# Second mixer: its convolution as column-group products, with TensorE in a written-out order

## The chip, the core and the metric

The kernel runs on one core of one Trainium2 chip. The metric is the device time of one execution in microseconds (us). Times of instructions are those of one execution recorded by the hardware profiler. TensorE (PE in the rows) multiplies, with PEld its weight loads; VectorE (DVE) and ScalarE (ACT) do the elementwise work; GpSimd (POOL) does small powers; SyncE (SP) issues the weight transfers.

## What is computed

Two networks run one after the other on 256 rows of width 1024. The first has a state-space mixer, a feed-forward block, an attention mixer and another feed-forward block. The second puts 16 meta rows ahead of the 256 rows, runs one mixer and then a block with 16,384 experts. Only the second network's mixer is touched by the change. Cut to what matters:

```python
def conv_group(a, b, conv_w, conv_b, g_ln, b_ln):          # 512 channels, 31 taps
    h = a * jax.nn.sigmoid(b)
    h = lax.conv_general_dilated(h, conv_w[:, None, :], window_strides=(1,),
                                 padding=[(CONV_K - 1, 0)], feature_group_count=CONV_CH, ...) + conv_b
    h = layernorm(h, g_ln, b_ln)
    return jax.nn.silu(h)

z = rmsnorm_2(h, g_mix_norm) @ w_in
conv_out = conv_group(z[..., :512], z[..., 512:1024], conv_w, conv_b, g_conv_ln, b_conv_ln)
attn_out = mla_group(z[..., 1024:1280], z[..., 1280:1408], z[..., 1408:], pos, ...)   # 8 heads, causal softmax
mixed = jnp.concatenate([rmsnorm_2(attn_out, g_out_attn), rmsnorm_2(conv_out, g_out_conv)], axis=-1)
h = h + mixed @ w_out
```

## The kernel before

Activations are kept transposed, 1024 features as 8 groups of 128 partitions by 256 rows (272 with the meta rows), and the rows are otherwise handled as two tiles of 128. Each weight piece of 128 x 1024 comes in over SyncE's queue into one of four buffers and is split by `weight` (line 120) into a high part (ScalarE, line 128) and a low part (VectorE, line 129). Each product is then three matmuls in a split-precision type: `mm_a` (lines 139 to 141, a weight piece as the stationary operand, 256 or 272 columns) or `mm_b` (lines 145 to 147, activations as the stationary operand, up to 512 columns). Attention, convolution and transposes run in plain f32; every f32 matmul is two records in the trace. `to_T` (line 164) transposes a tile on TensorE and splits it (lines 171, 133, 134).

`mix2` (line 782) is the stage of the change. `low_rank` (line 867) computes 416 columns of queries, keys, values and rotary part for three row tiles (two of 128 and one for the 16 meta rows); `ab(f)` (line 802) computes the gated values of 128 channels, for f from 0 to 3; `queries` and `key_values` expand the low-rank parts to 8 heads and turn them; `scores`, `flip` and `values` (lines 961 to 991) are one head's attention over one row tile, 16 in all; `attn_done` and `conv_done` norm the two halves and turn them into the operand `mT` of the output projection `out_proj` (line 239), which is 8 weight pieces, the first four for the attention half.

The convolution of a channel block is split. On TensorE, `taps_pe` builds a 128 x 128 diagonal for each tap on ScalarE (line 821) and multiplies it by a shifted view of the gated values (line 822). On VectorE, `taps_v` does one multiply-add per tap (line 829). The constant says how many taps TensorE has for each block:

```python
PE_TAPS = (4, 4, 6, 31)
```

So 45 taps are on TensorE and 79 on VectorE. The softmax of a row is two exponentials (lines 972 and 973), because the probabilities of the 16 meta keys are kept in a part of their own that is padded to 128; their sums are added by line 975.

The order is a planner's: the pieces are traced in an order that `weave` makes out of two lists, and a scheduler then orders every engine's queue by its own estimate of when operands are ready. `defer` and `tick` move the second half of a norm some pieces later. The stage ends:

```python
run(low_rank() + B[0])
weave([queries] + B[1] + [key_values], C[0])
weave(S, B[2] + C[1] + B[3] + C[2])      # S: attention, C: taps, B: ab
load_gain("ffn2_g")
run(C[3])
flush()
o = out_proj(A["w_out2"], KD, mT, keep_tiles(sb, 3, "qT2"))
conv_done(0)
conv_done(1)
```

## Time and profile before

| | |
|---|---|
| median of 3 runs | 1710.59 us (1710.31 to 1714.95) |
| the profiled execution, its own time | 1710.3 us |
| its span, first to last instruction | 1708.5 us |
| TensorE busy | 1669.0 us (98%) |
| VectorE busy | 1259.0 us (74%) |
| ScalarE busy | 964.7 us (56%) |
| mean granted TensorE clock | 0.996 of full |

The span is what the instructions cover; 1.8 us lie around it. Busy times of TensorE overlap, since a matmul's record runs to its modelled end while the next has begun: the distance from one start to the next tells what a matmul costs the queue. The second mixer runs from 777.5 us to about 900 us.

### The profile page before, as it was taken

Reading aid. Unit: us, or ns where it says so; the run is one execution under the profiler, and the core shown is the slowest. Engines: PE = TensorE matmul, PEld = TensorE weight load, DVE = VectorE, ACT = ScalarE, POOL = GpSimd, SP = SyncE. Lnnn points to the kernel's source line nnn. Section 1 sums busy time; section 2 is a strip of 40 time slices with the busy share of each in tenths; the row PEclk is TensorE's granted clock in tenths of the full one; section 3 lists DMA queues with packets and bytes.
Section 4 is the critical chain, followed back from the end, with each engine's and each line's share of the span. In section 5 each row is a group of like instructions: output and inputs, shape, how many; then the busy total and the mean of one; then the engine's idle time right before and its main releaser. Section 6 shows DMA issues by size and latency. Waiting matters only on the chain.

```text
span 1708.5 us, 28836 instructions
## 1 busy us (share of the span) xinstructions
PE 1669.0 (98%) x11003; PEld 1488.0 (87%) x11003; DVE 1259.0 (74%) x2581; ACT 964.7 (56%) x1425; POOL 37.6 (2%) x49
## 2 busy tenths in 40 slices
PE   6999999999999999999999999999999999999998
PEld 6978779997777799988988999999999888888886
DVE  5777667765765677757986998999999766666665
ACT  5688556544455665546765454556666544444443
POOL 0000000000100000001000000000000000000000
PEclk9999999999999999999999999999999999999999
DMA  5534445566354356664334666765555677777774
GB/s 192 183 119 141 136 148 182 188 197 199 118 177 134 116 174 185 208 212 145 103 99 160 229 221 218 230 226 174 182 177 178 214 239 237 235 232 242 237 241 151
DMA packets 88492, 315.30 MB, mean 185 GB/s; under 512 B 10001, under 2 KB 11409, under 8 KB 88225
## 3 DMA queue, kind: packets, MB, share of 16 engines
q1 hardware_dynamic: 80352, 290.36, 53.1%
q10 hardware_dynamic: 8000, 23.09, 3.7%
q8 instruction: 86, 1.41, 0.3%
q14 instruction: 54, 0.43, 0.1%
HBM read 295.59 MB, written 17.83 MB: 183 GB/s over the span
## 4 chain that ended last, share of the span: by engine, by line
PE 90%; DVE 4%; ACT 2%; issue 1%; DMA 1%; POOL 1%; SPq 0%; DVEq 0%; POOLq 0%; ACTq 0%
PE mm L1265 21%; PE mm L139 13%; PE mm L141 13%; PE mm L140 13%; PE mm L145 7%; PE mm L146 7%; PE mm L147 7%; PE pst L1224 3%; PE pst L171 1%; DVE lo L129 1%; PE pst L724 1%; PE pst L546 1%; PE po L749 1%; PE mm L822 1%; ACT hi L128 0%
## 5 line engine op out<-in xcount | busy, mean ns | idle before, releaser
L129 DVE TENSOR_TENSOR lo<-raw,hi 128x1024 fp32r<-128x1024 f32 (+1 forms) x492 | 599.6, 1220 | 289.6 <-PE mm L1265 81.2
L128 ACT ACTIVATE hi<-raw 128x1024 fp32r<-128x1024 f32 (+1 forms) x492 | 519.4, 1057 | 496.9 <-PE mm L140 220.8
L139 PE MATMUL mm<-xT,hi 128*128 128x256 f32 (+1 forms) x1968 | 562.3, 286 | 1.2 <-DVE cacc L320 1.2
L141 PE MATMUL mm<-xT,lo 128*128 128x256 f32 (+1 forms) x1968 | 556.6, 283 | 1.9 <-DVE lo L129 1.9
L140 PE MATMUL mm<-xT,hi 128*128 128x256 f32 (+1 forms) x1968 | 551.2, 280 | 0.0
L139 PEld LDWEIGHTS mm<-xT,hi 128*128 128x128 f32 x1968 | 371.5, 189 | 3.9 <-issue 2.3
L141 PEld LDWEIGHTS mm<-xT,lo 128*128 128x128 f32 x1968 | 370.1, 188 | 2.9 <-DVE lo L129 2.5
L140 PEld LDWEIGHTS mm<-xT,hi 128*128 128x128 f32 x1968 | 371.1, 189 | 0.7
L1265 PE MATMUL mm<-hi,xT 128*128 128x512 f32 x992 | 270.0, 393 | 0.0
L1265 PEld LDWEIGHTS mm<-hi,xT 128*128 128x128 f32 x992 | 186.3, 188 | 42.6
L1265 PE MATMUL mm<-lo,xT 128*128 128x512 f32 x496 | 154.7, 392 | 0.0
L1265 PEld LDWEIGHTS mm<-lo,xT 128*128 128x128 f32 x496 | 93.1, 188 | 21.6
L145 PE MATMUL mm<-hi,xT 128*128 128x512 f32 (+1 forms) x240 | 95.9, 406 | 4.4 <-ACT xT L133 3.8
L146 PE MATMUL mm<-lo,xT 128*128 128x512 f32 (+1 forms) x240 | 95.7, 399 | 2.2 <-DVE lo L129 2.2
L147 PE MATMUL mm<-hi,xT 128*128 128x512 f32 (+1 forms) x240 | 94.8, 396 | 2.1 <-DVE xT L134 2.1
L320 DVE SCALAR_TENSOR_TENSOR cacc<-mm,pcol,cacc 128x255 f32<-128x255 f32 (+1 forms) x144 | 68.4, 480 | 12.9 <-ACT cacc L317 10.4
L1225 ACT ACTIVATE G<-pst 128x512 f32<-128x512 f32 x64 | 68.3, 1106 | 0.0
L1215 DVE TENSOR_TENSOR oo<-oo,slot 128x1536 bf16<-128x1536 bf16 x64 | 61.2, 956 | 1.7
L145 PEld LDWEIGHTS mm<-hi,xT 128*128 128x128 f32 x240 | 45.2, 190 | 14.5 <-ACT xT L133 5.4
L147 PEld LDWEIGHTS mm<-hi,xT 128*128 128x128 f32 x240 | 45.3, 189 | 12.2 <-DVE xT L134 4.1
L146 PEld LDWEIGHTS mm<-lo,xT 128*128 128x128 f32 x240 | 45.5, 190 | 11.5 <-DVE lo L129 4.0
L145 PE MATMUL mm<-hi,aT 128*128 128x512 f32 x136 | 53.9, 396 | 0.0
(409 smaller groups left out, 2115.0 us busy)
## 6 DMA issues: line engine op xcount, KB each, us to landing
raw<-in_u SPq DMA_DIRECT2D x128, 512.0 KB, 4.1
raw<-in_v SPq DMA_DIRECT2D x128, 512.0 KB, 4.3
raw<-in_w_up SPq DMA_DIRECT2D x88, 512.0 KB, 3.6
raw<-in_w_dn SPq DMA_DIRECT2D x44, 512.0 KB, 4.2
raw<-in_w_fox SPq DMA_DIRECT2D x32, 512.0 KB, 4.2
spill<-h ACTq DMA_DIRECT2D x30, 512.0 KB, 5.5
h<-spill SPq DMA_DIRECT2D x30, 512.0 KB, 4.8
raw<-in_w_xbc SPq DMA_DIRECT2D x24, 512.0 KB, 3.7
```

The source lines that it names most:

```text
L128: last[1] = nc.scalar.activation(hi[:, :width], raw[:, :width], AF.Copy)
L129: last[0] = nc.vector.tensor_tensor(lo[:, :width], raw[:, :width], hi[:, :width].bitcast(F32), op=OP.subtract)
L139: nc.tensor.matmul(ps, lhsT=hi[:, k, :], rhs=xT[:, k, 0, :], start=(k == 0), stop=False)
L140: nc.tensor.matmul(ps, lhsT=hi[:, k, :], rhs=xT[:, k, 1, :], start=False, stop=False)
L141: nc.tensor.matmul(ps, lhsT=lo[:, k, :], rhs=xT[:, k, 0, :], start=False, stop=(k == nk - 1))
L145: nc.tensor.matmul(ps, lhsT=xT[:, k, 0, c0:c1], rhs=whi, start=first, stop=False)
L146: nc.tensor.matmul(ps, lhsT=xT[:, k, 0, c0:c1], rhs=wlo, start=False, stop=False)
L147: nc.tensor.matmul(ps, lhsT=xT[:, k, 1, c0:c1], rhs=whi, start=False, stop=last)
L320: nc.vector.scalar_tensor_tensor(acc[:, d:], ps[:, :T - d], cw[:, j:j + 1], acc[:, d:], op0=OP.mult, op1=OP.add)
L1215: nc.vector.tensor_tensor(oo[:, 2:], oo[:, 1:2].to_broadcast([P, 3, P, NB]), cur[:, 2:, None].to_broadcast([P, 3, P, NB]), op=OP.mult)
L1225: nc.scalar.activation(G[:, :, t0:t0 + NB].rearrange("p i t -> p t i"), pg, AF.Copy)
L1265: nc.tensor.matmul(acc[2 * t + c], lhsT=w[x][:, t * P:(t + 1) * P], rhs=y[:, c, :], start=(i == 0 and x == 0 and y is b[0]), stop=(i == P ...
```

## The change

The convolution moves to TensorE as a whole. Each block of 128 channels is handled as four column groups of 32 channels. The gated values are written to DRAM and read back as four copies shifted by one row each, laid out so that the 128 partitions of one operand are 32 channels times 4 shifts; one matmul with a stationary operand of 128 x 32 does four taps of 32 channels, and its output goes to 32 of the 128 PSUM partitions. Eight such steps cover 32 taps (31 and a zero). The stationary tables are laid out on the host side of the layout function, like the weights, and come from DRAM in two transfers, so that ScalarE builds no diagonals and VectorE has no taps.

The softmax becomes one exponential over the whole row: the first block of keys is taken as 128 columns that overlap the next, and the values of the meta tile are zero beyond row 16. The low-rank projection computes for the meta tile only the 160 columns that are used. TensorE's queue is in program order for the stage (`manual_schedule`), with an explicit list `fill` of what stands between the attention steps. Weight pieces are loaded and split one ahead of use (`plan`, `pre`). The output projection takes the four convolution pieces first, and two of them are placed in attention steps 16 and 17. The diff, cut to its core:

```diff
-PE_TAPS = (4, 4, 6, 31)
-CD = 0
+NTAP = 8
+CD = 1
...
+    pre, plan = [], []
+
     def weight(src, shape, width=PIECE, keep=None):
+        if pre:
+            s, w = pre.pop()
+        else:
+            w = load(src, shape, width, keep)
+        if plan:
+            pre.append((plan[0][0], load(*plan.pop(0))))
+        return w
...
-    def out_proj(src, nk, yT, keep, fin=residual):
+    def out_proj(src, nk, yT, keep, fin=residual, order=None):
+        order = order or list(range(nk))
...
+            def diagonals():
+                for p in range(2):
+                    d = sb.tile([P, 2, 4 * NTAP, 32], F32, name=f"dg{p}")
+                    nc.scalar.dma_start(d, A["c2d"][p])
+                    DG[2 * p], DG[2 * p + 1] = d[:, 0], d[:, 1]
...
                     pb = a_block(A["w_ab"][f, 1], xT)
...
-                    nc.vector.tensor_tensor(U[f][:, CONV_K - 1:], pre[0], sg, op=OP.mult)
+                    nc.vector.tensor_tensor(u[:, CONV_K - 1:UW - 1], first[0], sg, op=OP.mult)
+
+                    d = dram.tile([P, UW], F32, name=f"cud{f}")
+                    nc.gpsimd.dma_start(d, u)
+                    V[f] = sb.tile([P, 4, UW - 3 - NM], F32, name="cv", bufs=2)
+                    for s in range(4):
+                        nc.gpsimd.dma_start(V[f][32 * s:32 * s + 32],
+                                            d[:, NM + s:UW - 3 + s].rearrange("(q c) t -> c q t", q=4))
...
-            def taps_pe(f, j0, j1):
+            def taps(f, m0, m1):
+                if m0 == 0:
                     CP[f] = ps_mm.tile([P, 512], F32, name="mm")[:, :T]
-                dg = sb.tile([P, j1 - j0, P], F32, name="dg", bufs=2)
-                for j in range(j0, j1):
-                    nc.scalar.activation(dg[:, j - j0, :], ident, AF.Copy, scale=col("c2w", f * CONV_K + j))
-                    nc.tensor.matmul(CP[f], lhsT=dg[:, j - j0, :], rhs=U[f][:, NM + j:NM + j + T], start=(j == 0),
-                                     stop=(j == PE_TAPS[f] - 1))
+                for m in range(m0, m1):
+                    for q in range(4):
+                        nc.tensor.matmul(CP[f][32 * q:32 * q + 32], lhsT=DG[f][:, q * NTAP + m],
+                                         rhs=V[f][:, q, 4 * m:4 * m + T], start=(m == 0), stop=(m == NTAP - 1))
...
-            def taps_v(f, j0, j1):
-                for j in range(j0, j1):
-                    nc.vector.scalar_tensor_tensor(cT[:, f, :], U[f][:, NM + j:NM + j + T], col("c2w", f * CONV_K + j),
-                                                   cT[:, f, :], op0=OP.mult, op1=OP.add)
...
-                            mm_b(acc[i][:, :416], xT, k, tiles[i], hi[:, j, :], lo[:, j, :], k == 0, k == KD - 1)
+                            n0 = 256 if i == 2 else 0
+                            mm_b(acc[i][:, n0:416], xT, k, tiles[i], hi[:, j, n0:], lo[:, j, n0:], k == 0, k == KD - 1)
...
-                            norm_later(z[:, :256], cq, gq, 1, lambda a, i=i: to_T(a, 2, cqT, i * P))
+                            norm_later(z[:, :256], cq, gq, 2, lambda a, i=i: to_T(a, 2, cqT, i * P))
...
-                nc.scalar.activation(za[:, :NM], z[:, :NM], AF.Exp, scale=-1.0, bias=mx, accum_out=r2[:, :1])
-                nc.scalar.activation(za[:, P:P + n - NM], z[:, NM:n], AF.Exp, scale=-1.0, bias=mx,
-                                     accum_out=r2[:, 1:])
-                nc.vector.tensor_tensor(rs[:, i, hh:hh + 1], r2[:, :1], r2[:, 1:], op=OP.add)
+                nc.scalar.activation(z[:, :n], z[:, :n], AF.Exp, scale=-1.0, bias=mx, accum_out=rs[:, i, hh:hh + 1])
...
-            run(low_rank() + B[0])
-            weave([queries] + B[1] + [key_values], C[0])
-            weave(S, B[2] + C[1] + B[3] + C[2])
+            order = [4, 5, 6, 7, 0, 1, 2, 3]
+            keep = keep_tiles(sb, 3, "qT2", "dg0", "dg1")
+            lr = low_rank()
+            lr[0]()
+            es.enter_context(tc.manual_schedule(engines={mybir.EngineType.PE}))
+            ab_pieces = [[(A["w_ab"][f, a], KD) for a in range(2)] for f in range(4)]
+            plan.extend([(A["w_c2"][3], 2, 832)] + ab_pieces[0] + ab_pieces[1] + ...)
+            diagonals()
+            run(lr[1:] + B[0] + B[1] + [queries, B[2][0], key_values, turn_q, B[2][1], turn_k])
+            mT = sb.tile([P, KD, 2, T], F32R, name="mT")
+            o = out_proj(A["w_out2"], KD, mT, keep, order=order)
+
+            fill = {0: B[3][:1], 1: [lambda: taps(0, 0, 4)], 2: [lambda: taps(0, 4, 8)], 3: B[3][1:],
+                    4: [lambda: taps(1, 0, 4)], 5: [lambda: taps(1, 4, 8)], 6: [lambda: taps(2, 0, 4)],
+                    7: [lambda: taps(2, 4, 8)], 8: [lambda: taps(3, 0, 4)], 9: [lambda: taps(3, 4, 8)],
+                    10: [lambda: conv_done(0)], 11: [lambda: conv_done(1)], 16: o[:1], 17: o[1:2]}
+            for j in range(19):
+                if j < 16:
+                    scores(j // 8, j % 8)
+                run(fill.get(j, [lambda: None]))
+                if 0 <= j - 2 < 16:
+                    flip((j - 2) // 8, (j - 2) % 8)
+                if 0 <= j - 3 < 16:
+                    values((j - 3) // 8, (j - 3) % 8)
+                    if j - 3 in (7, 15):
+                        attn_done((j - 3) // 8)
             load_gain("ffn2_g")
-            run(C[3])
-            flush()
-            o = out_proj(A["w_out2"], KD, mT, keep_tiles(sb, 3, "qT2"))
-            conv_done(0)
-            conv_done(1)
-            run(o[:4])
+            run(o[2:4])
             flush()
             run(o[4:])
```

`turn_q` and `turn_k` are the transposes that stood inside `queries` and `key_values`.

## Rows read from the trace of the kernel before

**Rows 1.** The page, part 1: busy us (share of the span) and instructions by engine.

```profile
PE 1669.0 (98%) x11003; PEld 1488.0 (87%) x11003; DVE 1259.0 (74%) x2581; ACT 964.7 (56%) x1425; POOL 37.6 (2%) x49
```

**Rows 2.** Windows: stretch, length, PE, PEld, DVE, ACT, POOL busy, clock, DMA.

```profile
777.50:898.30 120.80, 118.16 (x727) 104.50 (x726) 100.12 (x262) 83.66 (x227) 8.02 (x12) 1.00 0.36 117
803.10:825.40 22.30, 22.13 (x146) 19.37 (x145) 20.52 (x48) 17.14 (x40) 0.00 (x0) 1.00 0.40 124
```

**Rows 3.** Groups by line, 777.5 to 898.3: count | busy us, mean ns | idle before.

```profile
L822 PE MATMUL mm<-cu,dg 128*128 128x256 f32 x90 | 21.8, 382 | 0.0
...
L829 DVE SCALAR_TENSOR_TENSOR cT<-cu,pcol,cT 128x256 f32<-128x256 f32 x79 | 37.4, 481 | 0.7
```

**Rows 4.** TensorE timeline, 864.8 to 874.9: start us, busy us, instruction [idle before].

```profile
870.03 0.63 PE L171 MATMUL pst<-ident,on 128*128 128x128 f32 x4 [0.23 <-DVE on L862]
870.50 4.48 PE L822 MATMUL mm<-cu,dg 128*128 128x256 f32 x20
874.82 0.27 PE L1017 MATMUL pst<-ident,cT 128*128 128x128 f32 x1
```

**Rows 5.** TensorE timeline around one pair of line 724.

```profile
493.39 0.71 PE L724 MATMUL pst<-qkT,qkT 64*128 64x128 f32 x4
494.02 0.50 PE L145 MATMUL mm<-hi,xT 128*128 128x512 f32 x1
```

**Rows 6.** TensorE timeline where two pairs of line 724 met.

```profile
471.11 0.72 PE L724 MATMUL pst<-qkT,qkT 64*128 64x128 f32 x8
471.76 0.50 PE L146 MATMUL mm<-lo,xT 128*128 128x512 f32 x1
472.10 0.40 PE L147 MATMUL mm<-hi,xT 128*128 128x512 f32 x1
```

**Rows 7.** TensorE timeline of one attention step over the second row tile.

```profile
850.57 0.62 PE L964 MATMUL pst<-kT,qT 96*128 96x272 f32 x2
851.03 0.49 PE L981 MATMUL pst<-ident,za 128*128 128x128 f32 x3
851.36 0.78 PE L989 MATMUL po<-v,pT 128*128 128x64 f32 x6
851.98 0.43 PE L822 MATMUL mm<-cu,dg 128*128 128x256 f32 x1
```

**Rows 8.** TensorE timeline at the head of the stage.

```profile
781.35 0.35 PE L145 MATMUL mm<-hi,xT 128*128 128x416 f32 x1
781.54 0.35 PE L146 MATMUL mm<-lo,xT 128*128 128x416 f32 x1
...
783.62 0.63 PE L171 MATMUL pst<-ident,hn 128*128 128x128 f32 x4 [0.21 <-DVE hn L209]
784.00 0.44 PE L146 MATMUL mm<-lo,xT 128*128 128x416 f32 x1
784.28 0.63 PE L171 MATMUL pst<-ident,hn 128*128 128x128 f32 x4
...
799.26 0.41 PE L171 MATMUL pst<-ident,cq 128*128 128x128 f32 x2 [0.62 <-DVE rtmp L848]
```

**Rows 9.** Groups by line on VectorE, 777.5 to 898.3, as in rows 3.

```profile
L968 DVE CUSTOM_DVE_ANT_0 zz<-pst,amask 128x272 f32<-128x272 f32 x8 | 3.5, 436 | 0.3 <-PE pst L964 0.2
...
L862 DVE SCALAR_TENSOR_TENSOR on<-ln,nr,row_oconv_g 128x512 f32<-128x512 f32 x2 | 1.5, 752 | 0.6 <-POOL nr L859 0.4
...
L1032 DVE SCALAR_TENSOR_TENSOR ln<-on,ln 128x512 f32<-128x512 f32 x2 | 1.4, 681 | 0.0
...
L968 DVE DVE_READ_ACCUMULATOR2_ANT mx<- 128x1 f32 x16 | 1.3, 83 | 0.0
```

**Rows 10.** DMA issues: transfer, queue, count, KB each, median us to landing.

```profile
spill<-h ACTq DMA_DIRECT2D x30, 512.0 KB, 5.5
...
rope<-in_rope ACTq DMA_DIRECT2D x1, 48.0 KB, 1.7
```

More of the change, by code (lines that the diff above doesn't have):

```diff
@@ L118, in tile_body, with load @@
     last, crit = [None, None], [None, None]
+    pre, plan = [], []
     def weight(src, shape, width=PIECE, keep=None):
+        if pre:
+            s, w = pre.pop()
+            assert (s.tensor.name, s.offset) == (src.tensor.name, src.offset)
+        else:
[3 more added lines that the diff above has]
+        return w
+    def load(src, shape, width=PIECE, keep=None):
+        keep = keep() if callable(keep) else keep
         raw = wraw.tile([P, PIECE], F32, name="raw")
@@ L251, in item @@
             h = j - (nk - len(keep))
-            w = weight(src[j], 2, keep=keep[h]() if h >= 0 else None)
+            w = weight(src[order[j]], 2, keep=keep[h] if h >= 0 else None)
             mms(j, w, 0)
@@ L827, in taps_v @@
[L827 to L835 removed]
+                    u = sb.tile([P, UW], F32, name="cu", bufs=2)
@@ L926, in queries, with turn_q @@
                     nc.vector.tensor_copy(q[:, :, HM:], qr)
+            def turn_q():
+                for t in range(2):
+                    q = Q[t]
                     for hq in range(0, 8, 4):
@@ L951, in key_values @@
                         nc.scalar.activation(kT[:, hq:hq + 4, c0:c0 + rows], pt[:96, :, :rows], AF.Copy)
-            mT = sb.tile([P, KD, 2, T], F32R, name="mT")
             scale = 96 ** -0.5
-            zs = [sb.tile([P, 3 * P], F32, name=f"za{b}") for b in range(3)]
-            for zt in zs:
-                nc.vector.memset(zt[:, NM:P], 0.0)
+            nc.vector.memset(v[:, 2], 0.0)
+            zs = {}
             rs = sb.tile([P, 2, 8], F32, name="rs")
@@ L998, in attn_done @@
                 on = sb.tile([P, 512], F32, name="on", bufs=2)
-                norm_later(o, on, og, 3, lambda a: to_T(a, 4, mT, i * P))
-            def attn_items():
-                out = []
-                for j in range(18):
-                    if j < 16:
-                        out.append(lambda i=j // 8, a=j % 8: scores(i, a))
-                    if 0 < j < 17:
-                        out.append(lambda i=(j - 1) // 8, a=(j - 1) % 8: flip(i, a))
-                    if j > 1:
-                        out.append(lambda i=(j - 2) // 8, a=(j - 2) % 8: values(i, a))
-                        if j in (9, 17):
-                            out.append(lambda i=(j - 2) // 8: attn_done(i))
-                return out
+                norm_later(o, on, og, 3 if i == 0 else 1, lambda a: to_T(a, 4, mT, i * P))
             def conv_done(t):
@@ new lines, in mix2 @@
+            ab_pieces = [[(A["w_ab"][f, a], KD) for a in range(2)] for f in range(4)]
+            plan.extend([(A["w_c2"][3], 2, 832)] + ab_pieces[0] + ab_pieces[1] + [(A["w_uq"][k], 2, 768) for k in range(2)]
+                        + ab_pieces[2][:1] + [(A["w_ukv"], 2)] + ab_pieces[2][1:] + ab_pieces[3]
+                        + [(A["w_out2"][k], 2, PIECE, keep[j - 5] if j > 4 else None) for j, k in enumerate(order)])
+            diagonals()
+            run(lr[1:] + B[0] + B[1] + [queries, B[2][0], key_values, turn_q, B[2][1], turn_k])
@@ L1353, in _layout @@
     o["w_ukv"] = g["w_ukv_2"][0]
+    w = np.concatenate([g["conv_w_2"][0].reshape(CONV_K, 512), np.zeros((1, 512), np.float32)])
+    w = w.reshape(8, 4, 4, 4, 32).transpose(1, 4, 2, 3, 0)
+    d = np.zeros((4, 32, 4, 4, 8, 32), np.float32)
+    for c in range(32):
+        d[:, c, :, :, :, c] = w[:, c]
+    o["c2d"] = d.reshape(P, 2, 2, 32, 32).transpose(1, 0, 2, 3, 4)
     o["w_out2"] = g["w_out_2"][0].reshape(KD, P, D)
```

58 lines of the change are left out of this document (29 added, 29 removed).

## The prediction, made before the change was run

> **What bounds the kernel now.** I read the busy shares of the page first: TensorE is busy for 98% of the span and no other engine for more than 74% [rows 1], so a change counts by what it does to TensorE's queue. Only the second mixer changes, so the second view is the busy time by stretch of that stage, from its first transposes (777.5 us) to the last third of its output projection (898.3 us). There TensorE is busy for 118.2 of 120.8 us, at a granted clock of 1.00 (the 2.4 GHz level), while VectorE has 100.1 and ScalarE 83.7 us [rows 2]. The stage is bound by TensorE, with 2.6 us of idle time. Most of the work the diff removes is on VectorE and ScalarE: 79 tap operations of 0.481 us, 37.4 us, on VectorE [rows 3], and 45 scaled copies of the identity and half of the exponentials on ScalarE. That work already lies beside TensorE and is worth nothing by itself. The sum must be made on TensorE's queue, then corrected for stretches where the other two engines take longer than TensorE.
>
> A busy time of the page is no price here, since matmuls overlap in it. I take the distance between starts: 20 records of line 822 take the 4.32 us from 870.50 to 874.82, 0.216 us each [rows 4]. The trace has 90 such records for 45 taps [rows 3]: an f32 matmul is two records.
>
> **Part by part, on TensorE.**
>
> Old taps: 90 records x 0.216 = 19.4 us go.
>
> New taps: 4 channel blocks x 8 steps x 4 column groups = 128 products, 256 records, each again over 256 columns. One at a time they cost 256 x 0.216 = 55.3 us; four at a time 13.8; two at a time 27.6. No row of before uses column groups. The nearest rows use two halves of the array's rows: line 724 puts an even head on partitions 0 to 63 and an odd one on 64 to 127. Where one pair stood alone, four records took 493.39 to 494.02, 0.63 us [rows 5]; where an even and an odd pair met, eight took 471.11 to 471.76, 0.65 us [rows 6]. The second chain cost 0.02 us, though both have two records per product that must follow one another. So chains on disjoint parts of the array ran side by side here, and a chain waiting for its own second record did not hold up the other. I take four at a time, 13.8 us, and keep 27.6 and 55.3 as ends. The Trainium skill ("TensorE: Matmul & The Clock Gate", Part 3: Packing small matmuls) gives 3.07 times for four tiles, an estimate of 55.3 / 3.07 = 18.0 us in place of 13.8; no run here shows that figure.
>
> Changing the shape of the array: the lone block's four records are worth 4 x 0.11 (three transposes take 851.03 to 851.36 [rows 7]), so 0.2 us of its 0.63 is overhead, and 0.1 to 0.2 more lies around it (471.76 to 472.10 is long for one matmul [rows 6]). The new taps stand in 8 blocks of 16 products between full-width matmuls: 8 x 0.3 = 2.4 us (ends 0.8 and 3.2).
>
> Low-rank projection: the tile of the 16 meta rows is multiplied by 160 columns, not 416: 24 matmuls (8 k x 3). A 416-column one takes 0.19 us (781.35 to 781.54 [rows 8]). A short one does not fall below about 0.10: six records over 64 columns take 851.36 to 851.98 [rows 7]. 24 x 0.08 = 1.9 us; but half of it lies ahead of the second row tile's transposes, for which TensorE already waits at 783.62 [rows 8], so I count 1.0.
>
> Interleaving: after f32 work the first split-precision matmul takes 0.09 us more (784.00 to 784.28 against 0.19 [rows 8]). I count 32 such returns in the stage's timeline; in the written-out order I count 11. 21 x 0.09 = 1.8 us goes. The wait of 0.62 us for the normed query rows at 799.26 [rows 8] goes, since the transposes come a projection later; so does the 0.23 us at 870.03 [rows 4], where VectorE's taps delayed the attention norm. Together 0.9.
>
> So far: -19.4 + 13.8 + 2.4 - 1.0 - 1.8 - 0.9 = -6.9 us.
>
> **What comes back as waits.** The old schedule could fill any hole on TensorE with taps. In program order a late operand stops everything behind it: scores, transposes, values, taps and projection alike. Three places:
>
> (a) Queries to first scores, with keys and the two turns between. TensorE's own work there, without one channel block, is about 18.3 us; ScalarE's copies, weight splits and tanh are 17.6. The like stretch of before had ScalarE busy for 17.1 of 22.3 us [rows 2]. With both engines this full, and three PSUM buffers between the turns and their copies, I hand-placed the copies and found up to 3 us of waiting; half of that, 1.5, is taken (ends 0 and 3.0).
>
> (b) Attention steps 10 to 15. No taps are left as filler, so a step costs TensorE 850.57 to 851.98, 1.41 us [rows 7]; with 8 convolution transposes and 12 turns into the output operand the six steps have 10.7 us. VectorE must in that time do six score reductions (0.44 + 0.08 us), and per row tile of the convolution eight more operations, five of them on 128 x 512 at 0.68 to 0.75 us (statistics, the two of lines 1025 and 1028, lines 1032 and 862) [rows 9], 4.1 us; the first attention norm, 1.8; three splits of 0.69. 3.1 + 8.1 + 1.8 + 2.1 = 15.1 us. The output projection's first piece, placed at step 16, needs both convolution tiles, so TensorE waits for 5.2 us if VectorE must finish everything, and for about 1.5 if what the projection does not need (last reductions, last splits) slips behind. I take 3.5.
>
> (c) The gated values now go out to DRAM and back as four shifted copies, through POOL's queue, into two buffers. The last block's copy can start only when block 1's taps have released their buffer at the end of step 5, and its taps stand in step 8: two filled steps, about 6.9 us later. Landings in this trace take 1.7 to 5.5 us [rows 10]; POOL's own issue time no row shows. I take 0.5 (ends 0 and 5). POOL also computes the powers of the norms, but all of those in the stage's first half are ahead of the copies, and the later ones come after step 10. The Trainium skill ("SBUF — State Buffer") says that some VectorE operations keep POOL from writing descriptors until they end; no run here shows it, and it would push (c) toward its upper end.
>
> The 2 MB of tables are two transfers on ScalarE's queue at the head of the stage, are first read some 40 us later, and meet DMA engines that are busy for 0.36 of the stage [rows 2]: nothing. Weight pieces split one ahead cost nothing extra; without that cover each would cost a split, about 1.2 us. The single exponential and the earlier convolution rows take away ScalarE work and a tail that TensorE had covered: nothing.
>
> Sum: -6.9 + 1.5 + 3.5 + 0.5 = -1.4 us. The profiled execution took 1710.3 us, its span is 1708.5, and the median of the runs is 1710.59, so it is a typical one. 1710.3 - 1.4 = **1708.9 us**.
>
> **The rivals.** *The waits don't come* (faster): VectorE is nearly empty in steps 4 to 9, and if its order lets the projection's operands through first, TensorE's work is all there is: 1710.3 - 6.9 = 1703.4. For it: 2.6 us of idle time in the whole stage before. Against: 15.1 us of VectorE work beside 10.7.
>
> *Two at a time* (slower): matmuls start strictly in order, so a group's second record, waiting for its first, holds up the next group. Then a product advances the queue by one record, 128 x 0.216 = 27.6 us, 13.8 more than forecast: 1722.7. The turning point is about 21 us of taps: above that the kernel is over 0.3% slower. The Trainium skill ("TensorE: Matmul & The Clock Gate", Part 3) has it so: matmuls keep program order in start and end. The records of [rows 6] speak against it, for row halves, if the eight records stood in the queue pair by pair, which the trace does not tell.
>
> *Columns don't run side by side at all*, so that the change doesn't do what it says: 55.3 us, 1710.3 - 1.4 + 41.5 = 1750. Only the absence of any column row speaks for it.
>
> *All three waits at their upper ends* (slower): 5.2 + 3.0 + 5.0 in place of 5.5: 1716.6.
>
> **How the numbers follow.** Chances: forecast 0.42 (its own range 1704 to 1714), waits don't come 0.30, two at a time 0.12, waits at the upper ends 0.11, no overlap 0.05. A measurement can tell 0.3%, 5.1 us, from no change: faster means under 1705.2, slower over 1715.4. Faster: 0.28 of the second case and 0.06 of the forecast, 0.34. Slower: 0.05 + 0.12 + 0.09 = 0.26. Within: 0.40. The range leaves out the last case and tails of 0.06 or so on either side: below, the waits gone and the shape changes at their lower end with a little over; above, just past two at a time: 1700.5 to 1723.
>
> **What would show it.** Starts of the new tap records: four within some 0.05 us and the next four 0.216 later is right; pairs or singles mean the rivals. A block of 16 products should take 1.7 us plus 0.3. In steps 10 to 15 the transposes should wait for VectorE's lines of the norms, 3 to 4 us in all, and the turns before the first scores for ScalarE. Taps of the last block waiting for a DMA would show (c) too small. I am wrong if TensorE's idle time stays near 2.6 us, if a block takes over 2.5 us, or if the granted clock falls below 1.00 in a wait.

## The result, and the profile after

The changed kernel takes 1721.2 us (median of 10 runs, 1717.4 to 1726.7) against 1711.5 us before (10 runs on the same chip): a ratio of 1.0056, 95% interval 1.0045 to 1.0067. It is 9.7 us slower; the forecast was 1708.9 us. The profiled execution took 1725.0 us, near the top of the ten: its stage begins 3.3 us later (780.89 against 777.60 us), in work that the change does not touch, so only the stage is compared below. A median run is 3.8 us shorter than this one, so the losses below are those of one of the longer runs.

The page's first part answers rows 1. VectorE is 32 us and ScalarE 17 us lighter, as the diff promises, and TensorE is busy 4 us longer:

```profile
PE 1673.2 (97%) x11169; PEld 1485.4 (86%) x11169; DVE 1226.7 (71%) x2488; ACT 947.4 (55%) x1348; POOL 49.4 (3%) x69
```

The windows view answers rows 2: first the whole stage, then three stretches of it (columns as in rows 2).

```profile
780.90:914.80 133.90, 121.70 (x899) 100.47 (x898) 68.52 (x173) 67.76 (x152) 20.35 (x33) 0.95 0.45 144
786.00:792.00 6.00, 5.02 (x25) 4.64 (x25) 3.55 (x5) 1.19 (x2) 0.33 (x1) 0.72 0.58 168
861.00:867.00 6.00, 5.34 (x52) 3.48 (x56) 0.45 (x2) 0.38 (x1) 0.00 (x0) 0.72 0.00 0
883.00:891.00 8.00, 7.85 (x30) 6.83 (x31) 2.46 (x4) 1.62 (x5) 0.00 (x0) 0.57 0.18 66
```

The stage takes 133.9 us; before it took 122.7. TensorE idles for 12 us in it, though VectorE and ScalarE are each busy for about half of it, and the granted clock, 1.00 all through the stage before, falls to the 1.2 GHz level for parts of three stretches. Who ended TensorE's waits, from the list of waits of the stage (us in total, times, longest):

```profile
PE pst L185 <- DVE on L881: 2.9, 2, 1.5
PE pst L185 <- DVE cqT L148: 2.0, 1, 2.0
PE mm L851 <- DMA cv<-cud: 1.8, 1, 1.8
PE mm L161 <- DVE stat L245: 1.6, 1, 1.6
PE pst L185 <- DVE hn L223: 1.0, 1, 1.0
PE po L1019 <- ACT pT L1013: 0.6, 1, 0.6
PE pst L996 <- DVE mT L148: 0.5, 1, 0.5
PE pst L984 <- ACT kT L985: 0.5, 1, 0.5
```

To set the runs side by side I split each stage's length, from the first transposes of its normed input to those of the next stage, into three parts: *waits* (the gaps of over 0.08 us between TensorE's records), *clock* (the sum, over windows of 1 us, of TensorE's busy time times what the granted clock lacks to 1.00) and *own* (the remainder: TensorE's work at full clock).

| kernel | median us | ratio to before, interval | stage | waits | clock | own |
|---|---|---|---|---|---|---|
| before | 1711.5 | | 122.7 | 2.8 | 0 | 119.9 |
| changed | 1721.2 | 1.0056 (1.0045 to 1.0067) | 133.9 | 12.1 | 6.6 | 115.2 |
| e_planner | 1711.2 | 0.9998 (0.9989 to 1.0008) | 122.5 | 5.3 | 3.4 | 113.8 |
| e_groupwise | 1737.3 | one run | 148.8 | 10.5 | 1.7 | 136.6 |
| e_repeat | 1721.1 | 1.0058 (1.0044 to 1.0072) | 133.0 | 7.3 | 3.4 | 122.3 |
| e_freebuf | 1718.3 | 1.0041 (1.0028 to 1.0054) | 135.1 | 11.0 | 9.5 | 114.5 |
| e_early | 1724.3 | 1.0075 (1.0062 to 1.0088) | 135.8 | 12.1 | 10.4 | 113.3 |
| e_spread | 1719.7 | 1.0050 (1.0031 to 1.0069) | 128.7 | 10.9 | 3.1 | 114.6 |
| e_tanhbuf | 1725.3 | 1.0080 (1.0068 to 1.0093) | 135.2 | 12.0 | 8.6 | 114.6 |
| e_ownbuf | 1719.2 | 1.0045 (1.0031 to 1.0058) | 130.1 | 11.5 | 3.4 | 115.2 |
| e_nonorm | 1714.6 | 1.0035 (1.0014 to 1.0055) | 125.8 | 9.1 | 1.7 | 115.0 |
| e_tuned | 1723.1 | 1.0061 (1.0043 to 1.0079) | 134.8 | 10.2 | 9.8 | 114.8 |
| e_retimed | 1715.3 | 1.0029 (1.0020 to 1.0039) | 126.7 | 9.0 | 1.7 | 115.9 |
| e_retimed_planner | 1710.6 | 1.0001 (0.9992 to 1.0010) | 121.7 | 6.1 | 0 | 115.6 |
| e_late_planner | 1712.5 | 1.0008 (0.9999 to 1.0017) | 123.6 | 5.3 | 3.2 | 115.1 |
| e_front_planner | 1710.5 | 1.0003 (0.9990 to 1.0016) | 122.6 | 6.2 | 0 | 116.4 |

The ratio is to the kernel before as it ran beside each group of experiments, where its median lay between 1710.6 and 1711.5 us; it is worked out from the runs and not from the two medians. The last four columns are of one profiled execution each.

The line of the changed kernel is the answer to where the time went: TensorE's own work fell by 4.7 us, its waits grew by 9.2 us, and 6.6 us went to the half clock: 11.2 us in the stage of this execution. The ten runs vary with the clock, too: the quickest (1717.4 us) had a mean granted clock of 0.996, the slowest (1726.7 us) 0.991.

### The profile page after: what moved, and what is told of

It reads as the page before. It is cut to its first block, busy times and chain, and to the rows that moved or that the text cites. A ratio compares the mean times of both kernels' runs of the same rounds, so it can differ in the third digit from the quotient of the medians.

```text
span 1723.2 us, 29048 instructions
## 1 busy us (share of the span) xinstructions
PE 1673.2 (97%) x11169; PEld 1485.4 (86%) x11169; DVE 1226.7 (71%) x2488; ACT 947.4 (55%) x1348; POOL 49.4 (3%) x69
## 3 DMA queue, kind: packets, MB, share of 16 engines
q8 instruction: 87, 1.43, 0.3%
## 4 chain that ended last, share of the span: by engine, by line
PE 50%; issue 1%; DMA 1%; DVE 1%; ACT 0%; POOL 0%; DVEq 0%; POOLq 0%; ACTq 0%
PE mm L1301 21%; PE mm L153 8%; PE mm L155 7%; PE mm L154 7%; PE pst L1260 3%; PE mm L159 1%; PE mm L161 1%; PE mm L160 1%; PE mm L851 0%; PE pst L1145 0%; DMA cud<-cu 0%; PE po L1019 0%; PE pst L185 0%; DMA cv<-cud 0%; PE pst L996 0%
## 5 line engine op out<-in xcount | busy, mean ns | idle before, releaser
L143 DVE TENSOR_TENSOR lo<-raw,hi 128x1024 fp32r<-128x1024 f32 x492 | 599.7, 1220 | 312.5 <-PE mm L1301 86.3
L142 ACT ACTIVATE hi<-raw 128x1024 fp32r<-128x1024 f32 x492 | 519.2, 1057 | 516.9 <-PE mm L154 232.3
L159 PE MATMUL mm<-hi,xT 128*128 128x512 f32 (+2 forms) x240 | 95.8, 405 | 4.6 <-ACT xT L147 3.9
L160 PE MATMUL mm<-lo,xT 128*128 128x512 f32 (+2 forms) x240 | 95.8, 400 | 2.2 <-DVE lo L143 2.2
L161 PE MATMUL mm<-hi,xT 128*128 128x512 f32 (+2 forms) x240 | 94.5, 395 | 2.8 <-DVE stat L245 1.6
```

Source lines behind the costliest of these rows:

```text
L142: last[1] = nc.scalar.activation(hi[:, :width], raw[:, :width], AF.Copy)
L143: last[0] = nc.vector.tensor_tensor(lo[:, :width], raw[:, :width], hi[:, :width].bitcast(F32), op=OP.subtract)
L159: nc.tensor.matmul(ps, lhsT=xT[:, k, 0, c0:c1], rhs=whi, start=first, stop=False)
L160: nc.tensor.matmul(ps, lhsT=xT[:, k, 0, c0:c1], rhs=wlo, start=False, stop=False)
L161: nc.tensor.matmul(ps, lhsT=xT[:, k, 1, c0:c1], rhs=whi, start=False, stop=last)
```

## The experiments

My theory after this comparison: the mechanism on TensorE was right, and the loss is that of in-order waits and of the half clock behind them. Its rival: the column groups themselves cost more than they save.

**The order of the queue.** e_planner drops one line:

```diff
-            es.enter_context(tc.manual_schedule(engines={mybir.EngineType.PE}))
```

> Edit: the changed kernel without the written-out order of TensorE; the planner orders its queue as in the kernel before, all else stays. Theory A (in-order waits): the changed kernel's TensorE work is about 4.5 us shorter than before's, but it waits for some 12 us in the stage where before waited 2.6, and after three of the waits the granted clock is 0.50 for 2.5 to 6 us, about 6.5 us lost. With a free order the waits fall back to 3 us or so and the half clock goes with them: 1721.2 - 9 - 6.5 = about 1706 (1703 to 1711). Theory B (the column groups themselves cost more than they save): the order hardly matters, 1718 or more.

Measured 1711.2 us, 10 us below the changed kernel and equal to before. The written-out order costs those 10 us, so the rival falls. But 1706 was missed: 5.3 us of waits stayed (head of the stage 1.6, attention's end 2.2), and 3.4 us of clock. The single exponential, the weights one ahead and the order of the output projection stay in this run; no run takes one of them away alone.

**The column groups.** e_groupwise turns the two loops of the taps:

```diff
-                for m in range(m0, m1):
-                    for q in range(4):
+                for q in range(4):
+                    for m in range(m0, m1):
```

> Edit: in each half block of taps the products stand column group by column group (four in a row on the same 32 columns) and not step by step (four in a row on four groups). Theory four at a time: matmuls start in queue order, and a record waits for the one ahead on its own columns; side by side run then only the products where one group meets the next, and a half block takes about 32 x 0.216 = 6.9 us less 3 overlaps of 0.43, 5.6 us, in place of 0.93: about 37 us more in all, 1758. Rival (the order in the queue doesn't matter, the array takes what is ready): 1721.

The half block of taps in the changed kernel and in this one, from the timeline of TensorE (start, busy us, instruction):

```profile
839.15 1.93 PE L851 MATMUL mm<-cv,dg 128*32 128x256 f32 x32
841.01 0.51 PE L996 MATMUL pst<-kT,qT 96*128 96x144 f32 x2
```

```profile
841.79 4.59 PE L851 MATMUL mm<-cv,dg 128*32 128x256 f32 x32
846.31 0.44 PE L1011 MATMUL pst<-ident,zz 128*128 128x128 f32 x2
```

1.86 us against 4.52 us, eight times: 21.3 us, which is the difference in own work (136.6 to 115.2). So the order in the queue matters, as the first theory had it, but the step was too large: I expected 5.6 us a half block. The starts of the single records, which the timeline merges into one row, tell why. A record does not name its columns; I read the groups from the 0.216 us between the records of one chain. In the changed kernel they come in fours (839.148, .155, .162, .168; the next four at 839.388 to .408, then every 0.216 us). Here one group's records follow one another at 0.216 us (836.82, 837.06, .28, .49, .71, ...), and the next group's first starts at 837.713, beside the third of the four products of its predecessor and ahead of the fourth, which starts at 838.139. Two products at each meeting of groups run side by side and not one: 20 record times in place of 32, 20 x 0.216 = 4.3 us. The Trainium skill ("TensorE: Matmul & The Clock Gate", Part 3: Packing small matmuls) has matmuls start and end in program order; across column groups these records, read this way, do not.

**The clock.** e_repeat keeps TensorE busy ahead of three waits:

```diff
-                nc.tensor.matmul(sp[:, :n], lhsT=qT[:, hh, i * P:(i + 1) * P], rhs=kT[:, hh, :n], start=True, stop=True)
+                for _ in range({8: 8, 14: 6, 15: 6}.get(8 * i + hh, 1)):
+                    nc.tensor.matmul(sp[:, :n], lhsT=qT[:, hh, i * P:(i + 1) * P], rhs=kT[:, hh, :n], start=True, stop=True)
```

> Edit: the changed kernel, with the score product of attention steps 8, 14 and 15 issued 8, 6 and 6 times over (the same values are written again); each stands right ahead of a wait of TensorE (2.2, 1.8 and 1.9 us from one start to the next), and the 7, 5 and 5 extra products are worth some 1.6, 1.2 and 1.2 us at full clock. No work is left out. Theory A (the waits bring the clock down): TensorE is busy through the waits, the granted clock stays at 1.00 in 861 to 867 and 883 to 891 us, and the 1.7 + 3.4 us lost there come back: 1721.2 - 5.1 = 1716, or up to 1.5 more since the score reductions begin later. Rival (the clock falls for another reason): the same or up to 2 us slower, 1721 to 1723.

Windows of the changed kernel, then of this one; the clock is the third figure from the end:

```profile
856.00:866.00 10.00, 8.20 (x86) 5.37 (x85) 0.97 (x5) 2.67 (x8) 1.95 (x4) 0.83 0.25 60
...
876.00:886.00 10.00, 6.57 (x38) 5.46 (x38) 7.78 (x18) 7.32 (x18) 1.10 (x2) 0.85 0.07 21
886.00:896.00 10.00, 9.42 (x43) 7.64 (x43) 3.61 (x3) 3.87 (x6) 0.00 (x0) 0.81 0.28 93
```

```profile
856.00:866.00 10.00, 10.00 (x110) 6.65 (x105) 1.10 (x5) 2.77 (x9) 0.93 (x2) 1.00 0.22 60
...
876.00:886.00 10.00, 8.95 (x56) 7.74 (x55) 6.06 (x13) 5.53 (x14) 1.20 (x2) 1.00 0.00 1
886.00:896.00 10.00, 9.42 (x54) 7.87 (x53) 6.05 (x8) 5.61 (x8) 0.00 (x0) 1.00 0.64 205
```

The clock stayed at 1.00 where TensorE was kept busy, and from the first to the 37th product of the output projection it took 11.9 us and not 13.8. In the two stretches where nothing was added (780 to 790 and 800 to 810 us) it fell, to 0.83 and 0.85. Over all runs the mean granted clock was 0.994 to 0.997, against 0.991 to 0.996 of the ten runs of the changed kernel. The time did not move, though: own work rose by 7.1 us, about what the waits and the clock gave back (4.8 and 3.3). The extra products were mis-priced. In step 14 six of them take 2.81 us to the next start, 0.47 each, where the expectation had 0.24, the price of one of the two records:

```profile
874.65 2.97 PE L997 MATMUL pst<-kT,qT 96*128 96x272 f32 x12
877.46 1.04 PE L185 MATMUL pst<-ident,on 128*128 128x128 f32 x8
```

So the 17 cost 8.0 us and not 4.0. The first half of the expectation held; the time missed by 5 us and does not tell what the clock alone is worth. A wait does not always bring the clock down: e_groupwise had the waits of steps 14 and 15 to the tenth of a microsecond (1.4, 0.5, 1.5 us) with the clock at 1.00 throughout. What decides that is open.

**The copies through DRAM.** e_freebuf gives block 2's copies memory of their own, so that block 3's need not wait for block 1's taps:

```diff
+                    if f == 2:
+                        V[f] = sb.tile([P, 4 * T + 6 * P], F32, name="cqk")[:, :4 * (UW - 3 - NM)].rearrange(
+                            "p (q t) -> p q t", q=4)
+                    else:
                         V[f] = sb.tile([P, 4, UW - 3 - NM], F32, name="cv", bufs=2)
```

> Edit: the third channel block's shifted copies go into memory that the low-rank operands have left, so that the fourth block's copies wait for the taps of block 0 and not of block 1; all else as changed. Theory A: the gap of 2.2 us ahead of the fourth block's taps goes, and the stretch at half clock behind it (about 1.7 us lost) too: 1721.2 - 3.9 = 1717.3. Rival: VectorE's norms end last anyway in attention steps 14 and 15, so what is gained here is waited for there: 1720 to 1721.

The wait stayed, 2.1 us. 1718.3 us is lower, but its interval overlaps the changed kernel's, so no gain is shown. GpSimd's timeline of the changed kernel shows why, once the values of block 3 are ready (VectorE's line 835 ends at 849.25):

```profile
849.55 0.56 POOL L838 DMA_DIRECT2D cud<-cu  x1 [3.65 <-DVE cu L835]
855.77 2.18 POOL L841 DMA_DIRECT2D cv<-cud  x4 [5.66 <-DMA cud<-cu]
```

TensorE's timeline of the same kernel has the other end, with the half clock in the length of the taps (2.79 us to the next start, not 1.86):

```profile
859.18 0.68 PE L996 MATMUL pst<-kT,qT 96*128 96x272 f32 x2
861.66 2.86 PE L851 MATMUL mm<-cv,dg 128*32 128x256 f32 x32 [1.80 <-DMA cv<-cud]
864.45 0.69 PE L1011 MATMUL pst<-ident,zz 128*128 128x128 f32 x2
```

The copies wait for the write to land (5.66 us), not for a buffer; then come four issues (2.18) and a second landing, 12.4 us from the values to the first tap. The freed buffer does not touch that; an earlier start of the values or a quicker landing would. Block 2's write landed after 3.1 us in the same kernel (the last section says what stood beside each). e_early, which keeps the freed buffer, tried taps, norms and pieces at other steps, and e_spread, on top of it, the low-rank transposes over three items and full-width products in the first two low-rank pieces:

```diff
-            fill = {0: B[3][:1], 1: [lambda: taps(0, 0, 4)], 2: [lambda: taps(0, 4, 8)], 3: B[3][1:],
...
-                    10: [lambda: conv_done(0)], 11: [lambda: conv_done(1)], 16: o[:1], 17: o[1:2]}
+            fill = {0: B[3][:1], 1: [lambda: taps(0, 0, 8)], 2: B[3][1:], 3: [lambda: taps(1, 0, 8)],
+                    4: [lambda: taps(2, 0, 8)], 6: [lambda: taps(3, 0, 8)], 7: [lambda: conv_done(0)],
+                    8: [lambda: conv_done(1)], 14: o[:1], 16: o[1:2]}
```

> Edit: as the run with the freed buffer, and the attention steps are filled in another way: whole blocks of taps in steps 1, 3, 4 and 6, the second gated half of block 3 in step 2, the convolution norms in steps 7 and 8 (10 and 11 as changed), the first output piece in step 14 (16 as changed). Theory A: VectorE's norm work now lies over nine steps and not six, so the waits of 1.4, 0.5 and 1.5 us in steps 14 and 15 and the half clock behind them (3.4 us lost) go as well: 1717.3 - 6.8 = 1710.5. Rival: the fourth block's copies, with two filled steps from its gated values to its taps, come late and cost 2 to 4 us and half clock: 1714 to 1717. Theory B (VectorE isn't the cause in those steps): they stay, 1717.

> Edit: as the run with the early fill, and the five transposes of low-rank tiles are spread over three items (they stand together as changed, where TensorE waits 2.0 us for the buffers that VectorE's splits free), and the first two low-rank pieces multiply the meta tile by 416 columns again, so that the wait for the rows of the stage ahead begins later. Theory A: 2.0 us of wait and 1.7 us of half clock at the head go, 0.3 us of matmul work comes back where it isn't covered: about 3.4 below the run with the early fill, 1707. Rival: each of the waits moves to the next norm of VectorE, 1710.

The waits of e_early, then of e_spread:

```profile
PE mm L855 <- DMA cv<-cud: 2.9, 1, 2.9
PE pst L185 <- DVE nss L882: 2.8, 1, 2.8
PE pst L185 <- DVE cqk L148: 2.2, 2, 2.0
```

```profile
PE mm L855 <- DMA cv<-cud: 3.0, 1, 3.0
PE pst L185 <- DVE nss L882: 2.8, 1, 2.8
...
PE mm L159 <- DVE cu L835: 1.1, 1, 1.1
```

e_early missed by 14 us: the copies were late by 2.9 us, as its rival said, and the norm moved its wait with it. Conv norm and steps moved together, so the distance between them stayed what it was. e_spread did what it was for in its trace (the 2.2 us at the low-rank transposes are gone, 1.1 us of them back at the queries, 7.3 us less clock). Its median is 4.6 us below e_early's, 3.4 expected, but the two intervals overlap, so the gain in time is not shown.

**The norm in steps 14 and 15.** The changed kernel's timelines of TensorE and of ScalarE:

```profile
876.14 0.68 PE L996 MATMUL pst<-kT,qT 96*128 96x272 f32 x2
878.24 1.23 PE L185 MATMUL pst<-ident,on 128*128 128x128 f32 x8 [1.42 <-DVE on L881]
...
880.92 0.73 PE L996 MATMUL pst<-kT,qT 96*128 96x272 f32 x2 [0.51 <-DVE mT L148]
883.15 1.08 PE L185 MATMUL pst<-ident,on 128*128 128x128 f32 x4 [1.50 <-DVE on L881]
```

```profile
878.91 0.63 ACT L1048 ACTIVATE on<-ln 128x512 f32<-128x512 f32 x1 [0.83 <-PE pst L185]
```

The second tile's tangent waited for TensorE's transposes of the first, which freed its buffer. Is it the buffer, or the norm's length? The first added line is e_tanhbuf, the second e_ownbuf; the last two, in place of the norm up to `norm_later`, are e_nonorm:

```diff
-                    th = sb.tile([P, 512], F32, name="on", bufs=2)
+                    th = sb.tile([P, 512], F32, name="o2", bufs=1)
+                    th = sb.tile([P, 512], F32, name="th", bufs=1)
...
-                ln = sb.tile([P, 512], F32, name="ln", bufs=2)
+                cn = sb.tile([P, 512], F32, name="on", bufs=2)
+                nc.scalar.activation(cn, pc.rearrange("p a b -> p (a b)"), AF.Copy)
```

> Edit: the changed kernel, with the hyperbolic tangent of the convolution norm in the buffer o2 and not in one of the two buffers named on. In the changed kernel the second row tile's tangent began at 878.91, when TensorE's transposes at 878.24 had freed that buffer. Theory A' (the waits in steps 14 and 15 are a chain of buffers): the second tile's norm no longer waits for the first tile's transposes; the wait of 1.5 us in step 15 goes and the half clock behind it (3.4 us lost): 1721.2 - 4 = 1717. Theory A'' (VectorE's work as such is too much for these steps, as the prediction had it): it is busy without a break there, the wait stays within 0.5 us: 1720 to 1721.

> Edit: the changed kernel, with the tangent of the convolution norm in a buffer that nothing else uses (the buffer o2, tried before, belongs to the attention norm of the same steps, so that run made a new wait of 3.2 us in place of the one it removed). Theory A' (chain of buffers): the second tile's norm no longer waits for the first tile's transposes, the wait of 1.5 us in step 15 goes, with the 3.4 us lost at half clock behind it where that stretch comes: 1721.2 - 1.5 = 1719.7 to 1721.2 - 4.9 = 1716.3. Theory A'' (VectorE has too much to do there in any case): the wait keeps over 1 us, 1721.

> Edit: the changed kernel, TensorE in its written-out order, without the norm of the convolution rows: the layer norm, the SiLU and the last norm of that half are left out, and the rows are copied as they come to the operand of the output projection; all transposes and products of TensorE stay where they were. Theory A'' and A' (the chain of the norm makes the waits of steps 14 and 15): they go, 3.4 us, with up to 3.4 us lost at half clock behind them; the waits for the low-rank transposes (2 us) and for the copies (2 us) stay: 1721.2 - 3.4 = 1717.8 to 1721.2 - 6.8 = 1714.4. Rival (attention's own reductions and the attention norm make them): over 1.5 us of the waits stays, 1719 to 1721.

e_tanhbuf (1725.3 us) says nothing on the question, since o2 belongs to the attention norm of the same steps: the edit itself made a wait of 3.21 us. e_ownbuf also takes one of three buffers from the low-rank rows `ck`, and the wait for the low-rank transposes grew there from 2.0 to 2.9 us. Its waits in steps 14 and 15 were

```profile
876.63 1.23 PE L185 MATMUL pst<-ident,on 128*128 128x128 f32 x8 [2.12 <-DVE on L881]
...
879.77 0.72 PE L996 MATMUL pst<-kT,qT 96*128 96x272 f32 x2 [0.96 <-ACT pT L1013]
880.68 0.55 PE L185 MATMUL pst<-ident,on 128*128 128x128 f32 x3 [0.19 <-DVE mT L148]
```

The third wait went down to 0.19 us, the first two grew by most of that: 3.27 us against 3.43. The buffer set which wait, not their sum. The median, 1719.2 us, lies in the range of theory A', but its interval overlaps the changed kernel's. Without the norm (e_nonorm) 0.8 us of the 3.4 is left, and the waits for low rank and copies stay (2.0 and 1.6). The median falls by 6.6 us, within the 3.4 to 6.8 expected; two of the six runs were at 1722 and 1724, though, and the interval overlaps the changed kernel's, so the traces carry this and not the time. The convolution norm makes these waits: from the transposes of the first convolution tile (869.46) to its normed rows (878.75) it takes 9.3 us by the timelines of TensorE and VectorE, while the steps between them have some 1.5 us of TensorE work each. VectorE is busy for 8.98 of the 9.09 us from 869.66 to 878.75, and the first attention norm stands among that work (its line 881 at 877.35). e_nonorm takes the chain and VectorE's load away together, so it does not tell them apart.

**A better place for the pieces.** Five versions put it all together. e_tuned and e_retimed keep the written-out order; e_retimed_planner, e_late_planner and e_front_planner leave it out. e_retimed's core:

```diff
-                    norm_later(ln, cn, cg, 2 * CD, lambda a: to_T(a, 4, mT, t * P, k0=4), half=True)
+                    norm_later(ln, cn, cg, 4, lambda a: to_T(a, 4, mT, t * P, k0=4), half=True)
...
+            fill = {0: B[3][:1], 1: B[3][1:], 2: [lambda: taps(0, 0, 4)], 3: [lambda: taps(0, 4, 8)],
...
+                    7: [lambda: taps(3, 0, 4)], 8: [lambda: taps(3, 4, 8)],
+                    9: [lambda: conv_done(0)], 10: [lambda: conv_done(1)], 17: o[:1]}
```

> Edit: all together, TensorE still in a written-out order: low-rank transposes spread over three items, the first two low-rank pieces on 416 columns, blocks 2 and 3 of the gated values three items earlier, block 3's copies in the freed memory, taps in steps 0 to 6, convolution norms in steps 7 and 8 and their transposes 6 steps later (as changed 4), the tangent in a buffer of its own, the first output pieces in steps 15 and 16. Theory A: every wait that the changed kernel has beyond before's 2.6 us goes, and the half clock with them: 1721.2 - 3.4 (steps 14, 15) - 2.2 (copies) - 2 (low rank) - 5 to 6.5 (clock) = 1707 to 1709, below before by 0.1 to 0.2%. Rival: the turns ahead of the first scores, with ScalarE and TensorE both full, wait more now that no gated block stands among the steps, and the attention steps without filler are paced by the chain of reduction, exponential and turn: 1712 to 1716.

> Edit: TensorE in a written-out order, each wait of the changed kernel taken at its own cause: low-rank transposes spread over three items and the first two low-rank pieces on 416 columns (as the run with the spread transposes); block 3's gated values in steps 0 and 1, six steps ahead of its taps; taps in steps 2 to 8; convolution norms in steps 9 and 10 and their transposes in 15 and 16, the tangent in its own buffer; the first output piece in step 17, the next three after the loop; the first attention norm's transposes after step 17. Theory A: the waits of 2.0 (low rank), 2.2 (copies) and 3.4 us (steps 14, 15) go, with up to 6.5 us of half clock: 1721.2 - 7.6 - 5 = 1708.6 (1706 to 1712). Rival (in written-out order a wait only moves on): 1716 to 1721.

> Edit: the same pieces in the same traced order, but TensorE's queue ordered by the planner. Theory A: what is left of waits is filled by neighbouring work: 1706 to 1708, and not above the written-out order. Rival: the planner's estimates put the column groups or the norms elsewhere, and it stays where the changed kernel in the planner's order stood, 1711.

> Edit: the planner's order, with the pieces traced as in the changed kernel (taps in steps 1 to 9, convolution norms in 10 and 11), and four single causes taken away: spread low-rank transposes, 416 columns in the first two low-rank pieces, block 2's copies in the freed memory, the tangent in its own buffer. Theory A: of the 5.3 us of waits in the planner's order the 2.2 us of the attention norm's and the half clock behind it go: 1711.2 - 2.2 - 1.7 = 1707 to 1708. Rival (the waits at the end of the attention are those of the norm's length, with the taps done late nothing is left to fill them): 1710 to 1712.

> Edit: the planner's order, with all gated values computed ahead of the attention, the taps in steps 0 to 6, the convolution norms in 7 and 8, their transposes in 13 and 14 and the first output pieces in 15 and 16; the same four single causes taken away. Theory A: the norms have TensorE work of 12 steps and two output pieces beside them, VectorE's 22 us against TensorE's 21: the waits fall to before's 3 us: 1707 (1705 to 1709), below before. Rival: the steps without taps wait for reduction and exponential, 0.3 us a step, as in the run with retimed pieces: 1710 to 1711.

e_tuned took over the buffer o2, and values waited 3.04 us for the attention norm behind it; it tells nothing more. e_retimed is 5.9 us below the changed kernel, half of what was expected, and its interval lies clear of the changed kernel's. Low-rank transposes and copies no longer wait, but the queries (1.2 us) and the norm (2.5 us) do, and the steps without taps wait for reduction and exponential. The three planner versions lie at 1710.5 to 1712.5 us, each with an interval that holds 1.000: theory A's 1706 to 1708 (1705 to 1709 for the last) did not come. e_front_planner's waits:

```profile
PE mm L161 <- DVE stat L245: 1.4, 1, 1.4
PE mm L159 <- DVE cu L834: 1.3, 1, 1.3
PE pst L185 <- DVE nss L882: 1.2, 1, 1.2
PE pst L1001 <- ACT pT L1018: 1.2, 2, 0.6
```

Wherever the taps stand, early, in the middle or late, 5 to 6 us of waits stay, 2.5 to 3.4 us more than before had. No version beat the kernel before by more than a measurement can tell.

## Why the prediction was wrong, step by step

**The step that failed** is *What comes back as waits*, and the sum that used it. It added 5.5 us for three places and took 0.9 off for two old waits, 4.6 net; the waits grew by 9.2 us. The sum had no term at all for the half clock behind a wait; it took 6.6 us. The three places hold 6.2 us (3.4 in steps 14 and 15, 1.0 ahead of the first scores, 1.8 for the copies), not far from 5.5. The rest came where the sum had nothing, or a gain.

**Right: what bounds the stage, and the four column groups.** The relief of VectorE and ScalarE was worth nothing, as said. Four records start within 0.02 us and the next four 0.216 us later; eight half blocks of 1.86 us are 14.9 us, against 13.8 + 2.4 in the sum. *Two at a time* and *no overlap* are out. TensorE's own work fell by 4.7 us; the terms of the sum for it make 6.0 (6.9 less the 0.9 of waits). The taps gave 19.4 - 14.9 = 4.5, where the sum had 3.2.

**Right as work: the low-rank projection.** Three products of 160 columns take 0.29 us and the next of 416 takes 0.23 and not 0.19: 0.33 for 3 x 0.19, eight times 0.24, the 1.9 us of the sum before it was halved.

```profile
797.17 0.24 PE L159 MATMUL mm<-hi,xT 128*128 128x160 f32 x1
...
797.46 0.39 PE L159 MATMUL mm<-hi,xT 128*128 128x416 f32 x1
797.69 0.35 PE L160 MATMUL mm<-lo,xT 128*128 128x416 f32 x1
```

**Misread: interleaving, 1.8 us.** The returns were counted rightly, 32 before and 11 now. But most of the 0.09 us is given back by the instructions ahead: in rows 8 the four transposes from 783.62 take 0.38 us to the next start, where four at the 0.11 of rows 7 make 0.44. Some 0.03 us a return is left, 21 x 0.03 = 0.6 us.

**Missed: the attention steps themselves.** 4.5 + 1.9 + 0.6 = 7.0 us, and 4.7 were saved, so 2.3 us of work came back. Part of it shows in steps without taps, 1.65 and 1.50 us from one to the next, without a wait long enough to count, where the sum had the 1.41 of rows 7. What made them longer is open.

```profile
872.99 0.68 PE L996 MATMUL pst<-kT,qT 96*128 96x272 f32 x2
...
874.64 0.73 PE L996 MATMUL pst<-kT,qT 96*128 96x272 f32 x2
```

The next step starts at 876.14, shown above with the norm's waits.

**Right: (b).** The waits of steps 14 and 15 sum to 3.4 us (3.5 taken), and e_nonorm shows the named cause, VectorE's norms. **Right in size: (a) proper**, the turns ahead of the first scores, 0.3 + 0.5 + 0.2 us against 1.5 (0 to 3.0).

**Wrong: "the wait of 0.62 us for the normed query rows goes, since the transposes come a projection later".** They come later, but all five stand together, and three PSUM buffers are freed by VectorE's splits, one by one. The changed kernel's timeline of TensorE answers the last line of rows 8:

```profile
805.87 0.38 PE L185 MATMUL pst<-ident,cq 128*128 128x128 f32 x2
808.23 0.33 PE L185 MATMUL pst<-ident,ck 128*128 128x128 f32 x1 [1.97 <-DVE cqT L148]
808.77 0.33 PE L185 MATMUL pst<-ident,ck 128*128 128x128 f32 x1 [0.22 <-DVE ckT L148]
```

2.2 us in place of 0.62. e_spread took it away by spreading them.

**Mis-sized: (c).** 0.5 us taken, 1.8 measured. The binding wait was not for the buffer, as the step had it, but for a DRAM write to land before the read can be issued: two landings in a row and five issues, 12.4 us, where I had counted one landing of rows 10 from the buffer's release. A write that lands after 3.1 us, as block 2's did, would by this arithmetic leave no wait; no run tests it.

**Missed: the head.** I had seen that TensorE already waits there and halved the low-rank gain for it. But half of the products cut were those that ran beside VectorE's last work of the stage ahead. Rows 8 have 0.21 us at the second tile's transposes, now there are 0.98, and the wait ahead of them, 0.96 in the kernel before, is 1.62, together 1.43 us more. e_spread, with 416 columns there again, has 1.42 and 0.28, so the shorter products explain 0.9 of it. The changed kernel's rows:

```profile
784.63 0.53 PE L161 MATMUL mm<-hi,xT 128*128 128x416 f32 x2 [1.62 <-DVE stat L245]
...
787.26 0.96 PE L185 MATMUL pst<-ident,hn 128*128 128x128 f32 x4 [0.98 <-DVE hn L223]
787.87 0.69 PE L160 MATMUL mm<-lo,xT 128*128 128x416 f32 x1
```

**Missed, and the largest: the clock.** The sum took 1.00 all through and named a fall as what would prove it wrong, without a price. The last row above lasts 0.69 us where rows 8 have 0.44 for the same matmul (784.00). The stage lost 6.6 us so; in e_repeat's trace it is gone from the two stretches where TensorE was kept busy. The Trainium skill ("TensorE: Matmul & The Clock Gate", Part 1: HAM oscillation) describes a kernel that waits, restarts at half clock and waits again; the trace agrees in part (0.57 in the 8 us behind the wait of step 15; e_groupwise has the same wait without it), and the sum had no term for it.

Together, in the profiled stage: own work 1.3 us less saved than forecast, waits grown by 9.2 us and not by 5.5 - 0.9 = 4.6, so 4.6 more, clock 6.6. That is, within rounding, the 12.6 us between -1.4 and +11.2. None of the rivals is what happened. By number *two at a time* (1722.7) came nearest, and its mechanism is out. *Waits at the upper ends* (1716.6) had the right kind of loss, but in three places that stayed near their middle values. The measured 1721.2 us lies within 1700.5 to 1723 only because that range was drawn out to take in *two at a time*: luck.

## What to carry to other kernels

Price a wait on an in-order TensorE twice: once for its length, and once for the stretch at half clock that may follow it. Work that becomes cheap stops being cover: before counting a gain, look for the longest chain through the other engines that the removed work had hidden, and ask what stands beside it now. A price read from the distance between two starts can be paid back by the instruction ahead, so read both. Transfers through DRAM cost two landings and every issue between them, so start them by the producer's time, not by the buffer's.

## What the runs showed of the hardware that was not expected

Across column groups products start out of queue order, as their spacing tells: in e_groupwise the first product of the next 32 columns started at 837.713, ahead of the previous group's fourth, at 838.139. A write of 151.5 KB to DRAM from GpSimd's queue was waited for 3.15 us in one block of e_freebuf and 5.75 us in the next. The traces tell what stood beside it. Block 2's write landed after 3.0 to 3.4 us in the 13 kernels where a weight piece (512 KB), issued 1.0 us ahead, was all that was under way. Block 3's landed after 4.5 to 5.8 us in the 11 where a gain (512 KB, line 110, ScalarE's queue) had been issued too, 2.3 us ahead. No run moves the gain alone, so this is read and not tested. The same three waits cost 3.4 us of half clock in the changed kernel and none in e_groupwise.
